# Causal attention scores: two float32r products over 128 rows in place of one native float32 product over 64

## The chip, the cores and the metric

The kernel runs on one core of a Trainium2 chip. The metric is device time in microseconds (us) for one execution, the median of three. In the rows, PE is TensorE (PEld its weight loads), DVE VectorE, ACT ScalarE, POOL GpSimd and SP SyncE, which issues the weight transfers.

## The reference, cut to what matters

Two layers on 256 tokens of 1024 features. Each layer is a half-step SwiGLU FFN, a mixer and another half-step FFN. All of it is float32. The mixer runs two attentions on the same normalised input: NSA (8 query heads, 2 key groups, with a compressed, a selected and a window branch under per-head gates) and MoBA (8 heads with keys of their own).

```python
x = x + 0.5 * _swiglu(_rms(x, ffn1_norm[l]), ...)
h = _rms(x, mix_norm[l])
(q_a, g_a, kc, vc, ks_, vs_, kw, vw, q_b, k_b, v_b, gate_a, gate_b) = _split_cols(h @ w_in[l])
y_a = _nsa(...) @ w_branch_nsa[l]
y_b = _moba(q_b, k_b, v_b) @ w_branch_moba[l]
x = x + (jax.nn.sigmoid(gate_a) * y_a + jax.nn.sigmoid(gate_b) * y_b) @ w_out[l]
x = x + 0.5 * _swiglu(_rms(x, ffn2_norm[l]), ...)
# in _nsa; selected and window branch alike, and MoBA per head:
s = jnp.einsum('grqd,gqnkd->grqnk', qc, kg) * scale
p = _masked_softmax(s, mask, (-2, -1))
return jnp.einsum('grqnk,gqnkd->grqd', p.astype(vg.dtype), vg)
```

At 256 tokens the selected blocks, the window and MoBA's one block hold every token up to the query's own. So three attentions are plain causal ones over 64-wide heads, and NSA's selected and window branch share their queries and differ in keys and values (the two key sets).

## The kernel before, in words

**Weights.** They come in pieces of [128, 2048] float32 on SP's queue, three raw buffers deep. ACT casts each half piece to float32r (`split_hi`, L218), DVE subtracts to get the remainder (`split_lo`, L225). A float32r operand holds the high part of a float32; its remainder is a second operand. Every large product is three float32r products (`mm3`, L133): high by high, high by low, low by high.

**Order.** The program is written out in the order of emission; no scheduler moves it. `tick` (L140) runs after every `mm3`: it emits deferred work (`defer`), a weight split every third tick, and every third tick one step of the attention (`side_step`), a generator that waits for flags. So PE sees nine weight products, then one step of the attention, then nine products. Each engine works its queue in order.

**The attention of one layer.** `cb_rope` rotates queries and keys on DVE right after their projection (L464 to L473). `pairs_T` (L513) transposes them on PE, two heads to a transpose of 128 columns, four transposes to a PSUM bank, and ACT copies the bank to SBUF as float32. `attend` (L680) makes jobs: token tile 0 has 4 heads to a score bank (128 keys each), tile 1 has 2 heads (256 keys). A job has three stages, and `attend_all` (L637) puts into one step the scores of job i, the transposes of the probabilities of job i-1 and the value products of job i-2:

- s1: native float32 score products over the 64 rows of a head (L695), mask (L698), maximum (L700), and on ACT an exponential for each head (L703), which gives P;
- s2: transposes of P (L711), which ACT copies (L713);
- s3: products with the values (L720); after the last head the gate weights (L538 to L542) and the scaling on DVE.

NSA has 16 heads per tile (8 for either key set): 4 score banks for tile 0 and 8 for tile 1. MoBA has 2 and 4. `compressed` (L646) is a job of its own behind each NSA tile: scores over 15 compressed keys (L652), a softmax written out on DVE (L655 to L662) with one exponential on ACT, `cpt` (a transpose) and `co` (its value product). The projections that run meanwhile are the output gates and MoBA's q, k and v.

**Buffers.** Tiles of 8 KB per partition come from a ring of 14 (`s4`, L92). PSUM has two banks for each of four uses: long sums a0 and a1, transposes `tr`, scores `sc`.

Of the kernel before, what the change touches and what calls it, by code (L numbers as in the profile page):

```python
# [39 lines left out]


def constants():
    """Position tables and masks: they depend on shapes alone."""
# [19 lines left out]
    # sums the halves' rows (half, g, c) of the compressed hidden layer, for keys and for values  # L63
# [17 lines left out]
def hybrid_kernel(ctx: ExitStack, tc: tile.TileContext, T, out):  # L81
# [9 lines left out]

    def s4(name, shape, dt=F32):  # L92
        return p4.tile(shape, dt, name=name, tag="s4", bufs=14)
# [21 lines left out]
    def flush():  # L115
        while later and later[0][0] <= clock[0]:
# [12 lines left out]
    def side_until(flag):  # L129
        while flag not in flags:  # L130
            assert side_step(), flag

    def mm3(ps, x, w, start, stop):  # L133
        """One [128, 128] block of float32 activations times [128, N] of weights, in exact halves."""
# [71 lines left out]
    # the splits' order: halves of a piece, finer for the first piece  # L206
# [33 lines left out]
    def get(*keys):  # L240
        """The halves of the named pieces, the first of which is the oldest still in use."""
# [39 lines left out]
    kbd = const.tile([128, G, 2, 16], F32, name="kbd")  # L281
    nc.gpsimd.memset(kbd, 0.0)
# [10 lines left out]
    class Norm:  # L293
# [7 lines left out]
        def squares(self, t, c, n, i):  # L301
            """The i-th share of the sum of squares, from n features"""
# [3 lines left out]
        def trans(self, t, h, wait=1):  # L306
            """The transpose's halves of the tokens t, features h, scaled by the gains"""
# [13 lines left out]
        def root(self, t, n):  # L321
            """r = rsqrt(mean(x^2) + eps): a power, and a step of Newton's"""
# [20 lines left out]
    def transposes(pair, src):  # L343
        """[128 tokens, n * 128] -> its transpose's halves, [128, n, 128] each"""
# [22 lines left out]
    def finish(nrm, g, y, t, h, ps):  # L367
        """x += ps / 2, and the output's share"""
# [19 lines left out]
    def ffn(l, n, nrm):  # L388
        actT = []
# [4 lines left out]
        for f in range(F // 512):  # L394
            hl = [s4("aT" + nm, [128, 4, S], F32R) for nm in "hl"]
            actT += [[y[:, k] for y in hl] for k in range(4)]
# [17 lines left out]
        # the last 256: gates and ups side by side  # L414
        aT = s4("aT", [128, 2, 2, S], F32R)
        hl = [aT[:, j] for j in range(2)]
# [33 lines left out]
        for t in range(NT):  # L450
            for h in range(2):
# [4 lines left out]
                else:  # L456
                    residual(nxt, t, h, ps[t][h], 4 + t)
        return nxt

    def rope(dst, ps, r, t, n, tab, dup):  # L460
        """dst [128, n, (dup,) 64] = rope(r * ps [128, n, 64]) at token tile t."""
# [7 lines left out]
        if dup:  # L469
            nc.vector.tensor_add(dst, t1[:, :, None, :].to_broadcast([128, n, 2, HD]),  # L470
                                 t2[:, :, None, :].to_broadcast([128, n, 2, HD]))
        else:
            nc.vector.tensor_add(dst, t1, t2)  # L473

    def mixer(l, nrm):
        # small weights of the compressed branch, a row (half, dim) per partition
# [29 lines left out]
        qa = s4("qa", [128, NT, NH, HD])  # L506
        # compressed blocks: the dims (half, d) by position, then (keys or values, high or low, g, c)
# [384 lines left out]
```

## Time and profile before

| | |
|---|---|
| median of three runs | 1198.42 us (1197.92 to 1198.84) |
| span of the profiled execution | 1195.6 us |
| PE busy | 1180.3 us, 99% of the span |
| DVE, ACT, POOL busy | 713.7 (60%), 577.9 (48%), 32.2 us (3%) |
| granted TensorE clock, mean | 0.998 of full speed |
| transfers | 203.5 MB, 170 GB/s on average |

The span is what the profiler saw from the first to the last instruction, 2.8 us less than the median of the runs. Busy time of PE includes fill and drain of each product, which overlap with the next; the distance between two starts tells what a product costs in a stream.

### The profile page before, as it was taken

How to read it: one execution, taken by the hardware profiler on the slowest of the kernel's cores; microseconds unless marked ns; L12 is line 12 of the kernel's file. 1: busy time of each engine (PE TensorE's matmuls, PEld its weight loads, DVE VectorE, ACT ScalarE, POOL GpSimd, SP SyncE). 2: the span in 40 equal slices, each digit the busy share in tenths (PEclk: the TensorE clock that was granted, in tenths of full speed). 3: DMA queues.
4: the chain of work that ended last, by engine and by line, in shares of the span. 5: the costliest groups of instructions: out<-in, count | busy, mean ns of one | idle time of the engine just before them, and what ended most of it. 6: DMA issues, size and time to landing. Idle time of an engine off the chain costs nothing.

```text
span 1195.6 us, 14342 instructions
## 1 busy us (share of the span) xinstructions
PE 1180.3 (99%) x5685; PEld 974.3 (81%) x5685; DVE 713.7 (60%) x976; ACT 577.9 (48%) x911; POOL 32.2 (3%) x41
## 2 busy tenths in 40 slices
PE   7999999999999999999999999999999999999997
PEld 5888888987878888888888888888878788888885
DVE  6655546877647674555475455487765576655553
ACT  6544444465456364444355444346545555444332
POOL 1000000001100000000000000000001000000000
PEclk9999999999999999999999999999999999999999
DMA  7756463763243466555546555537424254755540
GB/s 262 249 172 209 142 243 89 202 212 106 89 158 108 156 225 192 192 169 202 197 148 205 188 194 185 188 116 211 160 91 131 97 177 136 251 176 179 187 180 35
DMA packets 103282, 203.52 MB, mean 170 GB/s; under 512 B 4496, under 2 KB 25184, under 8 KB 103216
## 3 DMA queue, kind: packets, MB, share of 16 engines
q1 hardware_dynamic: 102592, 201.77, 51.5%
q8 instruction: 44, 0.72, 0.3%
q10 hardware_dynamic: 384, 0.55, 0.1%
q0 software_dynamic: 240, 0.30, 0.1%
q14 instruction: 22, 0.18, 0.0%
HBM read 201.55 MB, written 1.05 MB: 169 GB/s over the span
## 4 chain that ended last, share of the span: by engine, by line
PE 98%; DMA 1%; issue 0%; DVE 0%; ACT 0%; SPq 0%; POOLq 0%; POOL 0%
PE pr L135 9%; PE pr L137 8%; PE pr L136 8%; PE dn L137 7%; PE dn L135 7%; PE dn L136 7%; PE u L135 6%; PE u L136 6%; PE u L137 6%; PE g L136 6%; PE g L135 6%; PE g L137 6%; PE s L695 3%; PE o L720 3%; PE pT L349 2%; PE pt L711 2%
## 5 line engine op out<-in xcount | busy, mean ns | idle before, releaser
L225 DVE TENSOR_TENSOR lo<-raw,hi 128x1024 fp32r<-128x1024 f32 (+3 forms) x386 | 454.9, 1204 | 190.8 <-ACT hi L218 190.5
L218 ACT CAST hi<-raw 128x1024 fp32r<-128x1024 f32 (+3 forms) x386 | 386.5, 1038 | 227.2 <-PE dn L137 92.8
L135 PE MATMUL g<-hi,hT 128*128 128x512 f32 x320 | 129.3, 404 | 1.1 <-ACT hi L218 1.1
L135 PE MATMUL pr<-hi,hT 128*128 128x512 f32 (+2 forms) x320 | 129.7, 405 | 0.0
L136 PE MATMUL g<-lo,hT 128*128 128x512 f32 x320 | 125.5, 392 | 0.3 <-DVE lo L225 0.3
L135 PE MATMUL dn<-hi,aTh 128*128 128x512 f32 x320 | 125.8, 393 | 0.0
L137 PE MATMUL g<-hi,hT 128*128 128x512 f32 x320 | 125.5, 392 | 0.0
L137 PE MATMUL dn<-hi,aTl 128*128 128x512 f32 x320 | 124.7, 390 | 0.0
L135 PE MATMUL u<-hi,hT 128*128 128x512 f32 x320 | 124.6, 389 | 0.0
L136 PE MATMUL u<-lo,hT 128*128 128x512 f32 x320 | 124.5, 389 | 0.0
L136 PE MATMUL dn<-lo,aTh 128*128 128x512 f32 x320 | 124.5, 389 | 0.0
L137 PE MATMUL u<-hi,hT 128*128 128x512 f32 x320 | 124.5, 389 | 0.0
L137 PE MATMUL pr<-hi,hT 128*128 128x512 f32 (+2 forms) x320 | 122.6, 383 | 0.0
L136 PE MATMUL pr<-lo,hT 128*128 128x512 f32 (+2 forms) x320 | 121.8, 381 | 0.0
L703 ACT ACTIVATE P<-s,m 128x128 f32<-128x128 f32 (+1 forms) x96 | 39.4, 419 | 73.1 <-DVE m L700 53.0
L351 DVE TENSOR_TENSOR aTl<-pT,aTh 128x512 fp32r<-128x512 f32 x40 | 27.7, 692 | 76.2 <-ACT aTh L350 76.2
L136 PEld LDWEIGHTS g<-lo,hT 128*128 128x128 f32 x320 | 60.6, 189 | 12.8 <-DVE lo L225 1.3
L135 PEld LDWEIGHTS g<-hi,hT 128*128 128x128 f32 x320 | 60.5, 189 | 12.7 <-ACT hi L218 1.5
L137 PEld LDWEIGHTS g<-hi,hT 128*128 128x128 f32 x320 | 60.4, 189 | 12.8
L137 PEld LDWEIGHTS dn<-hi,aTl 128*128 128x128 f32 x320 | 60.1, 188 | 12.6
L135 PEld LDWEIGHTS u<-hi,hT 128*128 128x128 f32 x320 | 60.1, 188 | 12.5
L137 PEld LDWEIGHTS u<-hi,hT 128*128 128x128 f32 x320 | 60.1, 188 | 12.5
(193 smaller groups left out, 1585.4 us busy)
## 6 DMA issues: line engine op xcount, KB each, us to landing
raw<-in_ffn_wd SPq DMA_DIRECT2D x44, 1024.0 KB, 5.0
raw<-in_ffn_wu SPq DMA_DIRECT2D x40, 1024.0 KB, 5.1
raw<-in_ffn_wg SPq DMA_DIRECT2D x38, 1024.0 KB, 5.1
raw<-in_w_in SPq DMA_DIRECT2D x32, 1024.0 KB, 5.0
raw<-in_w_out SPq DMA_DIRECT2D x8, 1024.0 KB, 5.2
raw<-in_ffn_wg SPq DMA_DIRECT2D x12, 512.0 KB, 4.0
raw<-in_ffn_wu SPq DMA_DIRECT2D x8, 512.0 KB, 5.0
raw<-in_w_branch_nsa SPq DMA_DIRECT2D x4, 1024.0 KB, 5.1
```

Source lines behind the costliest of these rows:

```text
L135: nc.tensor.matmul(ps, x[0], w[0], start=start, stop=False)
L136: nc.tensor.matmul(ps, x[0], w[1], start=False, stop=False)
L137: nc.tensor.matmul(ps, x[1], w[0], start=False, stop=stop)
L218: nc.scalar.copy(done[i][0][:, a], raws[i][:, a])
L225: nc.vector.tensor_sub(lo[:, a], raws[i][:, a], hi[:, a].bitcast(F32))
L349: nc.tensor.transpose(p[:, k], src[:, 128 * k:128 * k + 128], ident)
L351: defer(1, lambda: nc.vector.tensor_sub(lo, p, hi.bitcast(F32)))
L695: nc.tensor.matmul(sp[:, i], qT[r, h // 2, 128 * t:128 * t + 128], kT(h)[r, 0:128 * nk], start=True, stop=True)
L703: nc.scalar.activation(P[:, i].rearrange("p a b -> p (a b)"), sp[:, i], AF.Exp, bias=m[:, i:i + 1], accum_out=O["su"][:, h:h + 1])
L711: nc.tensor.transpose(pt[:, i * nk + c], st["P"][:, i, c], ident)
L720: nc.tensor.matmul(O["o"][:, h], st["pT"][:, i * nk + c], v(h, c), start=c == 0, stop=c == nk - 1)
```

## The change

The scores are computed from float32r halves. A query's high part lies on 64 rows and its remainder on the other 64; the keys' high parts lie twice, on both halves, and so do the keys' remainders. Two products over 128 rows, one with each, then add up in PSUM (`start=u == 0`). For NSA one product serves both key sets at once, so its bank holds items (head, key set) and its columns are doubled: 512 for tile 1, 256 for tile 0. MoBA has 256 and 128.

For this the rotation of the queries ends in a split (add on DVE, cast on ACT, remainder on DVE), `queries_T` transposes one head at a time, `keys_T` writes high part and remainder, and two key banks go into one step. MoBA's keys are written twice by the rotation. The gates of both key sets are applied at once to a group's four heads. Compressed scores become eight float32r products with the high part and remainder of the keys side by side, summed on DVE. `s4` gets 15 named slots that are given back by hand, a flag is raised two ticks after its projection, and `kbd` is no longer zeroed on POOL.

```diff
+    slots, held = list(range(15)), {}
-        return p4.tile(shape, dt, name=name, tag="s4", bufs=14)
+        i = slots.pop(0)
+        a = p4.tile(shape, dt, name=name, tag=f"s4_{i}", bufs=1)
+        held[id(a)] = i, a
+        return a
+    def drop(*tiles):
+        slots.extend(held.pop(id(a))[0] for a in tiles)
...
@@ rope
+        if split:
+            nc.vector.tensor_add(t1, t1, t2)
+            nc.scalar.copy(dst[:, :, 0], t1)
+            defer(1, lambda: nc.vector.tensor_sub(dst[:, :, 1], t1, dst[:, :, 0].bitcast(F32)))
...
@@ mixer
-            flags.add((l, flag))
+            defer(2, lambda: flags.add((l, flag)))
-        def pairs_T(src, n, d, need=None):
-            for a in range(0, n, 2):
-                p = bank("tr", "pQ", [128, 2, S])
+        def queries_T(src, d):
+            for t in range(NT):
+                d.append(s4("qT", [128, NH, 128], F32R))
+                for a in range(0, NH, 4):
+                    p = bank("tr", "pQ", [128, 4, 128])
+                    for i in range(4):
+                        nc.tensor.transpose(p[:, i], src[t][:, a + i].rearrange("p u d -> p (u d)").bitcast(F32), ident)
+                    nc.scalar.copy(d[t][:, a:a + 4], p)
+                drop(src[t])
+                yield None
+        def keys_T(src, pairs, hi, lo):
+            for a in range(pairs):
+                p = bank("tr", "pK2", [128, 2, S])
...
+                h = hi(a)
+                nc.scalar.copy(h, p)
+                defer(1, lambda a=a, h=h, p=p: nc.vector.tensor_sub(lo(a), p, h.bitcast(F32)))
+                if a % 2:
+                    yield None
...
@@ compressed, s1
-                for a in range(4):
-                    nc.tensor.matmul(sp[:, 2 * a:2 * a + 2, :], qT[:, a, 128 * t:128 * t + 128], kbd[:, a // 2],
-                                     start=True, stop=True)
+                for h in range(NH):
+                    nc.tensor.matmul(sp[:, h], qT[t][:, h], kbd[:, h // 4], start=True, stop=True)
-                nc.vector.tensor_add(s, sp, K["cneg"][:, t, None, :].to_broadcast([128, NH, 16]))
+                nc.vector.tensor_add(s, sp[:, :, 0], K["cneg"][:, t, None, :].to_broadcast([128, NH, 16]))
+                nc.vector.tensor_add(s, s, sp[:, :, 1])
...
@@ attend, s1
-                    for i, h in enumerate(heads):
-                        r = slice(64 * (h % 2), 64 * (h % 2) + 64)
-                        nc.tensor.matmul(sp[:, i], qT[r, h // 2, 128 * t:128 * t + 128], kT(h)[r, 0:128 * nk],
-                                         start=True, stop=True)
+                    for i in range(0, per, nj):
+                        h = some[i][0]
+                        for u in range(2):
+                            nc.tensor.matmul(sp[:, i:i + nj], qT[t][:, h], kT(h, u, 128 * nk), start=u == 0, stop=u == 1)
...
@@ attention
-            yield from pairs_T(ksd.rearrange("p t j g u d -> p t (j g) (u d)"), 4, ksT)
+            yield from keys_T(lambda t, i: ksd[:, t, i % 2, i // 2], G, lambda g: ks[0][:, g], lambda g: ks[1][:, g])
...
-            yield from pairs_T(qa.rearrange("p t (a u) d -> p t a (u d)", u=2), 4, qaT)
+            yield from queries_T(qa, qaT)
...
+                        a = scaled("aS", o, weights_of(su, gate[:, t, hs, 1:3])).rearrange("p (h j) d -> p h j d", j=2)
+                        nc.gpsimd.tensor_add(A[:, t, hs], a[:, :, 0], a[:, :, 1])
...
-            yield from pairs_T(qb[0].rearrange("p t (a u) d -> p t a (u d)", u=2), 4, qbT)
-            yield from pairs_T(kb[0].rearrange("p t (a u) d -> p t a (u d)", u=2), 4, kbT)
+            yield from queries_T(qb, qbT)
+            yield from keys_T(lambda t, i: kb[t][:, i], NH // 2, lambda a: half(0, a), lambda a: half(1, a))
```

How the queues stand after it. DVE, around the compressed softmax of NSA tile 0 in the first layer, before (`rt` and `qb` are the rotation of MoBA's first query tile, `cs` the compressed scores, `lo` a weight remainder, the last row the mask of the first bank of tile 1):

```order
L473 TENSOR_TENSOR qb<-rt_2190,rt_2192 128x512
L225 TENSOR_TENSOR lo<-raw,hi 128x1024
L655 TENSOR_TENSOR cs_2213<-cs,c_cneg 128x128
L657 TENSOR_REDUCE cm<-cs_2213 128x8
L658 TENSOR_TENSOR cs_2213<-cs_2213,cm 128x128
L660 TENSOR_TENSOR cs_2213<-cs_2213,c_cok 128x128
L662 TENSOR_REDUCE csu<-cs_2213 128x8
L539 TENSOR_SCALAR cf<-csu 128x8
L540 RECIPROCAL cf<-cf 128x8
L542 TENSOR_TENSOR cf<-cf,gate 128x8
L225 TENSOR_TENSOR lo<-raw,hi 128x1024
L698 TENSOR_TENSOR s<-s,c_causal 128x2x128
```

And after the change:

```order
L695 TENSOR_TENSOR cs_2222<-cs_2222,cm 128x128
L697 TENSOR_TENSOR cs_2222<-cs_2222,c_cok 128x128
L699 TENSOR_REDUCE csu<-cs_2222 128x8
L571 TENSOR_SCALAR cf<-csu 128x8
L572 RECIPROCAL cf<-cf 128x8
L578 TENSOR_TENSOR cf<-cf,gate 128x8
L477 SCALAR_TENSOR_TENSOR rt_2248<-pr,r,ropeq 128x512
L481 SCALAR_TENSOR_TENSOR rt_2250<-pr,r,ropeq 128x8x32 x2
L483 TENSOR_TENSOR rt_2248<-rt_2248,rt_2250 128x512
L485 TENSOR_TENSOR qb<-rt_2248,qb 128x8x64
L236 TENSOR_TENSOR lo<-raw,hi 128x1024
L735 TENSOR_TENSOR s<-s,c_causal 128x2x128
```

The rotation (`rt`, `qb`) stood ahead of the compressed softmax and stands behind it now, between it and the mask of the next bank, and its last row needs ACT's cast.

ACT at the same place, before (`P` is a bank's exponentials, `pT` the copy of its transposes, `cpT` that of the compressed ones, `hi` a weight cast):

```order
L218 CAST hi<-raw 128x1024
L659 ACTIVATE cs_2213<-cs_2213 128x128
L713 COPY pT<-pt 128x512
L703 ACTIVATE P,su<-s,m 128x256 x2
L669 COPY cpT<-cpt 128x128
L218 CAST hi<-raw 128x1024
L703 ACTIVATE P,su<-s,m 128x256 x2
```

And after:

```order
L229 CAST hi<-raw 128x1024
L696 ACTIVATE cs_2222<-cs_2222 128x128
L750 COPY pT<-pt 128x512
L484 CAST qb<-rt_2248 128x8x64
L229 CAST hi<-raw 128x1024
L740 ACTIVATE P,su<-s,m 128x256 x2
L706 COPY cpT<-cpt 128x128
L740 ACTIVATE P,su<-s,m 128x256 x2
L750 COPY pT<-pt 128x512
```

The casts of the two query tiles (`qb`) are new; the weight cast and the exponentials of the next banks of tile 1 stand behind them.

## Rows read from the trace of the kernel before

**Rows 1.** The page: part 1 (busy us, share, instructions), part 4 (share of the chain).
```profile
PE 1180.3 (99%) x5685; PEld 974.3 (81%) x5685; DVE 713.7 (60%) x976; ACT 577.9 (48%) x911; POOL 32.2 (3%) x41
...
PE 98%; DMA 1%; issue 0%; DVE 0%; ACT 0%; SPq 0%; POOLq 0%; POOL 0%
```

**Rows 2.** PE's timeline in the attention: start us, us, engine line op out<-in xcount.
```profile
261.29 0.40 PE L137 MATMUL pr<-hi,hT 128*128 128x512 f32 x1
...
262.71 0.65 PE L711 MATMUL pt<-c_ident,P 128*128 128x128 f32 x4
...
274.58 0.97 PE L652 MATMUL cs<-kbd,qaT 128*128 128x32 f32 x8
275.39 0.64 PE L711 MATMUL pt<-c_ident,P 128*128 128x128 f32 x4
...
278.60 0.39 PE L137 MATMUL pr<-hi,hT 128*128 128x512 f32 x1
278.92 1.13 PE L695 MATMUL s<-ksT,qaT 64*128 64x256 f32 x4
279.98 0.33 PE L667 MATMUL cpt<-c_ident,cs 128*128 128x128 f32 x1
...
284.28 0.66 PE L711 MATMUL pt<-c_ident,P 128*128 128x128 f32 x4
...
293.49 0.66 PE L711 MATMUL pt<-c_ident,P 128*128 128x128 f32 x4
```

**Rows 3.** The same timeline of PE around the hidden layer of the compressed branch.
```profile
241.54 0.40 PE L137 MATMUL pr<-hi,hT 128*128 128x512 f32 x1
241.77 0.28 PE L630 MATMUL hh<-hi,X 128*128 128x256 f32 x1
241.89 0.27 PE L630 MATMUL hh<-lo,X 128*128 128x256 f32 x1
...
246.02 0.60 PE L519 MATMUL pQ<-c_ident,qa 128*128 128x128 f32 x4
246.37 0.48 PE L135 MATMUL pr<-hi,hT 128*128 128x512 f32 x1
246.69 0.39 PE L136 MATMUL pr<-lo,hT 128*128 128x512 f32 x1
```

**Rows 4.** The timeline of DVE around the compressed softmax of NSA tile 0.
```profile
273.88 0.74 DVE L464 SCALAR_TENSOR_TENSOR rt<-pr,r,ropeq 128x512 f32<-128x512 f32 x1
...
276.05 1.22 DVE L225 TENSOR_TENSOR lo<-raw,hi 128x1024 fp32r<-128x1024 f32 x1
277.18 0.28 DVE L655 TENSOR_TENSOR cs<-cs,c_cneg 128x128 f32<-128x128 f32 x1
...
279.66 1.22 DVE L225 TENSOR_TENSOR lo<-raw,hi 128x1024 fp32r<-128x1024 f32 x1
280.80 0.43 DVE L698 TENSOR_TENSOR s<-s,c_causal 128x256 f32<-128x256 f32 x1
281.26 0.69 DVE L700 TENSOR_REDUCE m<-s 128x2 f32<-128x512 f32 x1
281.86 0.16 DVE L539 TENSOR_SCALAR cf<-su 128x8 f32<-128x8 f32 x1
...
282.57 0.69 DVE L533 TENSOR_TENSOR aS<-o,cf 128x512 f32<-128x512 f32 x1
```

**Rows 5.** The timeline of ACT: two of the exponentials.
```profile
262.25 0.21 ACT L703 ACTIVATION_READ_ACCUMULATOR P<-s,m 128x1 f32 x1
...
282.06 0.47 ACT L703 ACTIVATE P<-s,m 128x256 f32<-128x256 f32 x1 [3.13 <-DVE cf L539]
```

**Rows 6.** Groups by line, DVE and ACT: form xcount | busy us, mean ns | idle before.
```profile
L351 DVE TENSOR_TENSOR sl<-pT,sh 128x512 fp32r<-128x512 f32 x8 | 5.5, 690 | 8.2 <-ACT sh L350 8.2
...
L350 ACT CAST sh<-pT 128x512 fp32r<-128x512 f32 x8 | 4.7, 588 | 17.9 <-PE pT L349 17.9
```

**Rows 7.** Stretch: us, PE, PEld, DVE, ACT, POOL busy (x), clock, DMA share, GB/s.
```profile
258.00:320.00 62.00, 62.00 (x352) 49.16 (x350) 43.19 (x81) 32.71 (x94) 3.39 (x2) 1.00 0.27 86
```

More of the change, by code (lines that the diff above doesn't have):

```diff
@@ L113, in defer, with flush @@
         later.sort(key=lambda e: e[0])
-    def flush():
-        while later and later[0][0] <= clock[0]:
+    def flush(ahead=0):
+        while later and later[0][0] <= clock[0] + ahead:
             later.pop(0)[1]()
@@ L457, in ffn, with rope @@
                     residual(nxt, t, h, ps[t][h], 4 + t)
+        drop(*tiles)
         return nxt
-    def rope(dst, ps, r, t, n, tab, dup):
+    def rope(dst, ps, r, t, n, tab, split):
         C = tab[:, t, None, 0:HD].to_broadcast([128, n, HD])
@@ L505, in mixer @@
         vv = p2.tile([128, NT, 2, G * HD], F32, name="vv", tag="vv", bufs=1)
-        qa = s4("qa", [128, NT, NH, HD])
+        qa = [s4("qa", [128, NH, 2, HD], F32R) for _ in range(NT)]
         X2 = [s4("X2", [128, 8, 2, 2, G, 16], F32R) for _ in range(2)]
@@ L541, in weights_of @@
             if gt is not None:
-                nc.vector.tensor_mul(c, c, gt)
+                if len(gt.shape) == 3:
+                    c2 = c.rearrange("p (h j) -> p h j", j=2)
+                    nc.vector.tensor_mul(c2, c2, gt)
+                else:
+                    nc.vector.tensor_mul(c, c, gt)
             return c
@@ L616, in compress_more @@
             nc.tensor.transpose(kp.rearrange("p g c -> p (g c)"), kc2.rearrange("p u d -> p (u d)"), ident[:64, :64])
-            for u in range(2):
-                r = slice(64 * u, 64 * u + 64)
-                nc.scalar.copy(kbd[r, :, u, :], kp[r, :, 0:16])
+            nc.scalar.copy(kbd[:, :, 0], kp[:, :, 0:16])
+            nc.vector.tensor_sub(kbd[:, :, 1], kp[:, :, 0:16], kbd[:, :, 0].bitcast(F32))
         HH = sm.tile([128, 2, CMP_HIDDEN], F32, name="HH", bufs=1)
@@ L634, in hidden @@
             nc.scalar.copy(HH, ps)
+            drop(*X2)
             flags.add((l, "HH"))
@@ L676, in compressed, with attend, s1 @@
             return s1, s2_, s3
-        HEADS = [0, 2, 4, 6, 1, 3, 5, 7]
-        def attend(t, qT, kT, v, finish):
+        def attend(t, heads, nj, qT, kT, v, finish):
             nk = t + 1
             per = 4 // nk
+            items = [(h, j) for h in heads for j in range(nj)]
             O = {}
-            for h0 in range(0, NH, per):
-                heads = HEADS[h0:h0 + per]
+            for i0 in range(0, len(items), per):
+                some = items[i0:i0 + per]
                 st = {}
-                def s1(h0=h0, heads=heads, st=st):
-                    if h0 == 0:
+                def s1(i0=i0, some=some, st=st):
+                    if i0 == 0:
                         O["su"] = sm.tile([128, NH], F32, name="su")
                     sp = bank("sc", "s", [128, per, 128 * nk])
-                    for i, h in enumerate(heads):
-                        r = slice(64 * (h % 2), 64 * (h % 2) + 64)
-                        nc.tensor.matmul(sp[:, i], qT[r, h // 2, 128 * t:128 * t + 128], kT(h)[r, 0:128 * nk],
-                                         start=True, stop=True)
+                    for i in range(0, per, nj):
+                        h = some[i][0]
+                        for u in range(2):
+                            nc.tensor.matmul(sp[:, i:i + nj], qT[t][:, h], kT(h, u, 128 * nk), start=u == 0, stop=u == 1)
                     own = sp[:, :, 128 * t:128 * t + 128]
@@ L701, in s1 @@
                     P = s2("P", [128, per, nk, 128])
-                    for i, h in enumerate(heads):
+                    for i in range(per):
                         nc.scalar.activation(P[:, i].rearrange("p a b -> p (a b)"), sp[:, i], AF.Exp,
-                                             bias=m[:, i:i + 1], accum_out=O["su"][:, h:h + 1])
+                                             bias=m[:, i:i + 1], accum_out=O["su"][:, i0 + i:i0 + i + 1])
                     st["P"] = P
@@ L713, in s2_, with s3 @@
                     nc.scalar.copy(st["pT"], pt)
-                def s3(h0=h0, heads=heads, st=st):
-                    if h0 == 0:
+                def s3(i0=i0, some=some, st=st):
+                    if i0 == 0:
                         O["o"] = bank("a1", "o", [128, NH, HD])
-                    for i, h in enumerate(heads):
+                    for i, (h, j) in enumerate(some):
                         for c in range(nk):
-                            nc.tensor.matmul(O["o"][:, h], st["pT"][:, i * nk + c], v(h, c),
+                            nc.tensor.matmul(O["o"][:, i0 + i], st["pT"][:, i * nk + c], v(h, c, j),
                                              start=c == 0, stop=c == nk - 1)
-                    if h0 + per == NH:
+                    if i0 + per == len(items):
                         finish(O["o"], O["su"])
@@ L812, in mixer @@
             elif c0 == C_Q:
-                project_in(c0, cb_rope(qa, ropeq), "Q")
+                project_in(c0, cb_rope(lambda t: qa[t], ropeq, True), "Q")
             elif c0 == C_QB:
-                project_in(c0, cb_rope(qb[0], ropeq))
+                qb.extend(s4("qb", [128, NH, 2, HD], F32R) for _ in range(NT))
+                project_in(c0, cb_rope(lambda t: qb[t], ropeq, True))
             elif c0 == C_KB:
-                kb.append(s4("kb", [128, NT, NH, HD]))
-                project_in(c0, cb_rope(kb[0], K["rope"]), "KB")
+                kb.extend(s4("kb", [128, NH, 2, HD]) for _ in range(NT))
+                project_in(c0, cb_rope(lambda t: kb[t], K["rope"], False), "KB")
             else:
```

65 lines of the change are left out of this document (36 added, 29 removed).

## The prediction

> **What bounds the kernel now.** I read the page first: TensorE (PE) is busy for 99% of the span, and the chain of work that ended last is PE for 98% [rows 1]. So a microsecond taken from PE is a microsecond of the run, as long as nothing else becomes late, and the reader should keep two lists: what each PE instruction costs in its place, and how early the results arrive that PE will ask for. For the first I read the timeline of PE around a side step of the attention [rows 2], and around the hidden layer [rows 3], where float32r products of 256 columns run. A record's duration contains its fill and drain and overlaps the next one, so I price by the distance from one start to the next. For the second I read the timelines of VectorE (DVE) and ScalarE (ACT) in the same stretch [rows 4, 5], and the stretch's totals: DVE is busy 43 of 62 us, ACT 33, and the granted clock is 1.00, that is 2.4 GHz [rows 7].
>
> The profiled execution has a span of 1195.6 us; the median of the three runs is 1198.42 us, 2.8 us more. I subtract what follows from the median.
>
> **Part 1: the score products (gain).** A native float32 product over 64 rows leaves two records (x4 for the two heads at 278.92 [rows 2]). A bank of token tile 1 (two heads, 256 keys): from the last ordinary product at 278.60 to what follows the scores at 279.98 are 1.38 us, of which 0.23 us is the ordinary product itself [rows 2, 3]; the scores cost 1.15 us, a gap of 0.09 us ahead of them included. Ahead of the float32r products of 256 columns there is no such gap (241.54 to 241.77 is 0.23 us), and each costs 0.12 us [rows 3]. A bank of tile 0 (four heads, 128 keys): 261.29 to 262.71 less 0.23 is 1.19 us [rows 2]. After the change, per layer:
> - NSA, tile 1: 8 banks, two products of 512 columns each, 2 x 0.23 = 0.46 us. Saved 8 x 0.69 = 5.5 us.
> - NSA, tile 0: 4 banks, four products of 256 columns, 0.48 us. Saved 4 x 0.71 = 2.8 us.
> - MoBA, tile 1: 4 banks, four products of 256 columns. Saved 4 x 0.67 = 2.7 us.
> - MoBA, tile 0: 2 banks, eight products of only 128 columns. The trace has no float32r product this narrow. Low end: half of a 256-column one, 0.06 us. High end: a native one, 1.19 us less the gap for four, 0.27 us each. I take 0.11 us, the distance of the 128-column transposes (0.35 us for four, and what they delay behind them [rows 3]), since these too load new stationary data every time. 8 x 0.11 = 0.88 us; saved 2 x 0.31 = 0.6 us. The ends give +1.4 and -2.0 us.
> - Compressed scores: eight records before (0.81 us, 274.58 to 275.39 [rows 2]), eight products after; taken as 0, within 0.3 us.
>
> Sum 11.6 us per layer, 23.2 us for both.
>
> A place where a page differs: the transposes of 128 columns stand 0.11 us apart [rows 3]. The Trainium skill (TensorE: Matmul & The Clock Gate, section Back-to-back issue gap) gives about 81 ns for each of a stream of 128-column products and about 131 ns at 512 columns; by it the four MoBA banks of tile 0 would save another 0.9 us. The trace's 512-column products stand 0.23 us apart, not 0.13, so I stay with the rows.
>
> **Part 2: more transposes (loss).** Queries: 16 transposes where there were 8, for NSA and for MoBA; MoBA keys 16 for 8; NSA keys unchanged. That is 24 more per layer, 6 groups of four. A group at 246.02 delays the second ordinary product after it to 246.69; 0.67 less 0.23 is 0.44 us [rows 3]. 6 x 0.44 = 2.6 us per layer, 5.3 us in all. They are matched by copies out of PSUM at 0.59 us each on ACT and subtractions at 0.69 us on DVE [rows 6]: per layer ACT gets 10 more (four query halves, four query banks, two key banks), DVE four query remainders and six key remainders, two wider additions for the MoBA keys, and an addition per compressed tile. DVE has 19 us to spare in the 62 us [rows 7], so throughput is hidden; where they stand in the queue is not (part 3). Where two banks are transposed in one step, the next pair waits for both copies: 0.87 us of transposes and nine products (2.1 us) cover 1.2 us of copies, one weight split and the remainders. I cost these bank waits at nothing; without that cover it would be about 0.3 us at five places a layer.
>
> **Part 3: what is late next (loss).** PE now reaches the transposes of the probabilities P 0.7 us sooner at each step, while the softmax behind them isn't shorter.
> - First bank of NSA tile 0. Its last P ends at 262.46 (262.25 plus 0.21), the last of the four transposes starts 0.33 us after 262.71 [rows 2, 5]: 0.58 us to spare. The way there loses the 0.71 us of the next bank's scores and the 0.1 us gap behind its own. Wait: 0.3 us. In MoBA tile 0 the scores shrink by 0.3 us alone: none.
> - First bank of NSA tile 1. Here the order shows the trap. The NSA keys take one step fewer, so the attention runs a step ahead of the projections. The MoBA query rotation, which DVE did ahead of the compressed softmax, now lands between it and the scores of this bank, and it ends in a round trip: DVE adds, ACT casts, DVE subtracts. DVE, counted from the start of the compressed scores: 1.0 us until they can be read; the compressed softmax 2.5 us (277.18 to 279.66) plus 0.3 for the new addition; rotation 2.2 (273.88 to 276.05); cast and remainder 0.59 + 0.69 and two handovers, 1.4; weight remainder 1.1; mask 0.5; maximum to first P 0.8 [rows 4, 5, 6]; P itself 0.5. Sum 10.3 us. PE: 274.58 to 278.92 less the gap of 0.09, then 278.92 to 284.28 less 2 x 0.69 [rows 2]: 8.2 us. Wait: 2.1 us, and 0.2 more for the second P. Before, that P was done at 282.53 (282.06 plus 0.47), 1.75 us early.
> - Two steps on, the second query tile does it again. From that first P on, DVE owes gate weights 0.7, a scaling 0.6, weight remainder 1.1, mask and maximum 1.1, the compressed scaling 0.6, rotation 2.2, round trip 1.4, mask to first P 1.8: 9.5 us, less the 0.5 between maximum and transpose, 9.0. PE: 284.28 to 293.49 is 9.2, less 2 x 0.69, plus 0.2: 8.0 us. Wait: 1.0 us.
>
> Queued behind the cast on ACT are a weight cast and the P of the next bank; behind the remainder on DVE a weight remainder and the next mask. PE waits for both chains.
>
> Sum 3.6 us per layer, 7.2 us in all. Its lower end is nothing, if the handovers and the weight remainders fall better; its upper end 4.5 us per layer, with the bank waits.
>
> **Sum.** 23.2 - 5.3 - 7.2 = 10.7 us: 1198.4 - 10.7 = **1187.7 us**.
>
> **The rivals.**
> - A: no new waits. For it: DVE and ACT are busy 70% and 53% of the stretch [rows 7], and later banks leave time. Against it: the queue order above. 1198.4 - 17.9 = 1180.5 us.
> - B: float32r products of 128 columns run at the native pace of 0.27 us. For it: no row shows one. Against it: at 256 columns a float32r product costs 0.12 us [rows 3]. It takes 2.6 us per layer from part 1, and gives 1187.7 + 5.2 = 1192.9 us.
> - C, slower: the round trip DVE, ACT, DVE sets the pace of the attention instead of PE, so that PE waits at every bank of NSA tile 1. It decides from 8.95 us of waits per layer, 1.1 us at each of eight banks. At 1.5 us per bank it gives 1180.5 + 24 = 1204.5 us. For it: two of the banks wait 1 to 2 us already. Against it: the round trip is met only where a query rotation falls, twice in the stretch, and DVE idles 30% of it [rows 7].
> - D: the change doesn't do what it says, and a float32r product over 128 rows with these operands costs as much as a native one. Then each bank doubles, and 1.15 us are added at some 16 banks per layer: 1198.4 + 5.3 + 37 = 1241 us. The hidden layer's rows [rows 3] speak against it.
>
> **How the numbers follow.** Forecast with its waits (1184 to 1191) 0.61; A 0.17; B 0.14; C 0.06; D 0.02. The range holds the forecast, A and B, with their unknowns: 1180 to 1194 us. A measurement of this kernel can tell about 0.2%, 2.4 us: faster means under 1196.0, slower above 1200.8. The forecast, A and B with no more than 0.01 lost are faster: 0.91. C and D, less a little of C that ends level, are slower: 0.06. The same: 0.03.
>
> **What would show it.** In the profile after: score records half as many per product, 0.23 us apart at 512 columns and 0.12 at 256; at 128 columns 0.11 (B: 0.27). 24 more transposes per layer. Idle time of PE ahead of the P transposes, put down to ACT P, of some 7 us in total, the longest about 2 us at the first bank of NSA tile 1 in each layer; A if there is none, C if it stands at all eight banks. The page should still have PE at 98 to 99% and the FFNs unchanged. I am wrong if the span shrinks by under 4 us or over 19, or if the waits stand elsewhere, such as at PSUM banks of the transposes.

## The result, and the profile after

The changed kernel takes 1189.27 us (median of four runs, 1187.61 to 1191.56) where the kernel before takes 1198.32 beside it: a ratio of 0.9928, 95% interval 0.9916 to 0.9941. A second set of five runs gave 1189.18 us (1187.39 to 1189.95). The prediction was 1187.7, with a range of 1180 to 1194.

The profiled execution took 1187.61 us, with a span of 1185.5 us where before's was 1195.6. The page of after, parts 1 and 4, which answer to [rows 1]:

```profile
PE 1165.1 (98%) x5669; PEld 973.2 (82%) x5669; DVE 730.1 (62%) x1002; ACT 587.6 (50%) x929; POOL 37.4 (3%) x44
...
PE 95%; DVE 2%; ACT 1%; DMA 1%; issue 1%; SPq 0%; POOLq 0%; POOL 0%; ACTq 0%; DVEq 0%
```

PE is busy for 15.2 us less while the span shrank by 10.1, and the chain now runs through DVE and ACT for some 3%. So PE waits where it did not before. PE's timeline after, in the same stretch of layer 0 as [rows 2] (start, us, group; in brackets the idle time ahead of it and its releaser):

```profile
271.53 0.96 PE L689 MATMUL cs<-kbd,qT 128*128 128x32 f32 x8
272.34 0.66 PE L748 MATMUL pt<-c_ident,P 128*128 128x128 f32 x4
...
275.81 0.62 PE L733 MATMUL s<-ksT,qT 128*128 128x512 f32 x2
276.27 0.27 PE L704 MATMUL cpt<-c_ident,cs 128*128 128x128 f32 x1
...
279.35 0.62 PE L733 MATMUL s<-ksT,qT 128*128 128x512 f32 x2
281.88 0.90 PE L748 MATMUL pt<-c_ident,P 128*128 128x128 f32 x4 [1.91 <-ACT P L740]
282.62 1.02 PE L710 MATMUL co<-vbd,cpT 128*128 128x512 f32 x2
...
289.43 0.61 PE L733 MATMUL s<-ksT,qT 128*128 128x512 f32 x2
290.63 0.89 PE L748 MATMUL pt<-c_ident,P 128*128 128x128 f32 x4 [0.59 <-ACT P L740]
```

A bank's scores cost 0.46 us (275.81 to 276.27). At 279.35 and 289.43 the same two products are followed by 2.53 and 1.20 us: waits of 2.07 and 0.74 us for the first P. The transposes of P behind the first (`pt`) stretch to 0.74 us (281.88 to 282.62) from 0.43 elsewhere, since the bank's second P is 0.3 us later still.

The table of PE's waits in the whole run (us, times, longest), of PE and of its weight loads:

```profile
PE pt L748 <- ACT P L740: 4.4, 3, 1.9
```
```profile
PEld pt L748 <- ACT P L740: 8.0, 12, 2.3
PEld o L757 <- ACT pT L750: 1.7, 6, 0.3
```

No bank of the transposes of queries and keys (pQ, pK) stands in it. The stretch of [rows 7] after (us, then busy us of PE, PEld, DVE, ACT and POOL; granted clock, DMA share, GB/s) has 2.7 us less of PE and 5.1 more of DVE, at the same clock:

```profile
258.00:320.00 62.00, 59.31 (x337) 48.86 (x336) 48.27 (x92) 34.75 (x96) 7.80 (x5) 1.00 0.30 100
```

DVE in the same place, to be read against [rows 4]:

```profile
275.33 0.74 DVE L477 SCALAR_TENSOR_TENSOR rt<-pr,r,ropeq 128x512 f32<-128x512 f32 x1
275.99 0.87 DVE L481 SCALAR_TENSOR_TENSOR rt<-pr,r,ropeq 128x256 f32<-128x256 f32 x2
276.90 0.69 DVE L483 TENSOR_TENSOR rt<-rt,rt 128x512 f32<-128x512 f32 x1
278.27 0.69 DVE L485 TENSOR_TENSOR qb<-rt,qb 128x512 fp32r<-128x512 f32 x1 [0.69 <-ACT qb L484]
278.88 1.22 DVE L236 TENSOR_TENSOR lo<-raw,hi 128x1024 fp32r<-128x1024 f32 x1
280.02 0.43 DVE L735 TENSOR_TENSOR s<-s,c_causal 128x256 f32<-128x256 f32 x1
```

The bank scored at 275.81 was written at 276.4, but its mask starts at 280.02, and its P is what PE waits for until 281.88. Rotation, 0.69 us of idling for ACT's cast, the remainder and a weight remainder stand ahead of it. The same idling of 0.69 us comes back at the second query tile (288.16).

### The profile page after: what moved, and what is told of

Read it like the earlier page. It is cut to its first block, busy times and chain, and to the rows that moved or that the text cites. A ratio compares the mean times of both kernels' runs of the same rounds, so it can differ in the third digit from the quotient of the medians.

```text
span 1185.5 us, 14381 instructions
## 1 busy us (share of the span) xinstructions
PE 1165.1 (98%) x5669; PEld 973.2 (82%) x5669; DVE 730.1 (62%) x1002; ACT 587.6 (50%) x929; POOL 37.4 (3%) x44
## 4 chain that ended last, share of the span: by engine, by line
PE 95%; DVE 2%; ACT 1%; DMA 1%; issue 1%; SPq 0%; POOLq 0%; POOL 0%; ACTq 0%; DVEq 0%
PE pr L146 8%; PE pr L148 8%; PE pr L147 8%; PE dn L146 7%; PE dn L147 7%; PE dn L148 7%; PE u L146 6%; PE u L147 6%; PE u L148 6%; PE g L147 6%; PE g L148 6%; PE g L146 6%; PE o L757 2%; PE pT L359 2%; PE s L733 1%; PE pt L748 1%
## 5 line engine op out<-in xcount | busy, mean ns | idle before, releaser
L148 PEld LDWEIGHTS u<-hi,hT 128*128 128x128 f32 x320 | 60.1, 188 | 12.5
L146 PEld LDWEIGHTS u<-hi,hT 128*128 128x128 f32 x320 | 60.1, 188 | 12.5
L147 PEld LDWEIGHTS u<-lo,hT 128*128 128x128 f32 x320 | 60.1, 188 | 12.4
```

The source lines that it names most:

```text
L146: nc.tensor.matmul(ps, x[0], w[0], start=start, stop=False)
L147: nc.tensor.matmul(ps, x[0], w[1], start=False, stop=False)
L148: nc.tensor.matmul(ps, x[1], w[0], start=False, stop=stop)
```

## Experiments

The first theory, Q: the waits come from what DVE has queued between the compressed scores and the mask of the next bank, and an edit that takes x us out of that queue takes x us off the wait. Rival S: the shorter scores alone make PE wait. Rival R: the round trip DVE, ACT, DVE is the whole price. And, for the runs' spread, a clock theory: a long wait lets the granted clock fall in some executions.

**The keys in two steps.** The attention falls back one step against the projections, as it stood before the change:

```diff
-                if a % 2:
+                if a % 2 or pairs == 2:
                     yield None
```

> The NSA keys yield after each bank again, so the attention falls back to where it stood against the projections before the change; the scores, the transposes and the round trip of the queries' split stay. Theory Q (queue): the waits of TensorE at the first banks of NSA tile 1 (2.36 and 1.25 us in layer 0) come from what DVE has queued between the compressed scores and the mask, and any edit that takes x us out of that queue takes x us off the wait. Here the MoBA query rotation starts about 1.7 us sooner against the compressed scores, so the first wait falls from 2.4 to about 0.6 us, some 4 us in both layers: 1189.3 - 4 = 1185 us (1183 to 1187). Rival S (scores): TensorE waits because its scores are shorter, wherever the rotation stands: the waits stay within 0.5 us, 1188.5 to 1190. Rival R (round trip): the cast on ACT and the handovers are what is late; the rotation's place matters little and the wait goes along with it: 1188 to 1190. Clock: if the spread of the changed kernel (1187.6 to 1191.6, mean granted clock 0.998 to 0.996) comes from waits of over 2 us, the runs of this kernel agree within 1.5 us at 0.998.

Measured: 1190.8 us median (1188.2 to 1191.62), no gain, where theory Q as I had put it gave 1183 to 1187. PE's timeline of this kernel shows why:

```profile
277.90 0.61 PE L733 MATMUL s<-ksT,qT 128*128 128x512 f32 x2
279.82 0.30 PE L704 MATMUL cpt<-c_ident,cs 128*128 128x128 f32 x1 [1.31 <-DVE cs L697]
...
282.96 0.62 PE L733 MATMUL s<-ksT,qT 128*128 128x512 f32 x2
283.55 0.90 PE L748 MATMUL pt<-c_ident,P 128*128 128x128 f32 x4
...
287.21 0.61 PE L733 MATMUL s<-ksT,qT 128*128 128x512 f32 x2
289.45 0.89 PE L748 MATMUL pt<-c_ident,P 128*128 128x128 f32 x4 [1.62 <-ACT P L740]
```

The wait of 2.07 us for the first P is down to 0.13 (282.96 to 283.55 is 0.59, less 0.46). But the rotation now stands ahead of the compressed softmax, and `cpt` waits for that instead: 277.90 to 279.82 is 1.92, less 0.46, 1.46 us. The second rotation falls between two masks and costs 1.78 us (289.45 less 287.21 less 0.46) where it cost 0.74. So the place of the rotation against the projections decides where the waits stand; here it did not lessen their sum, since at both new places PE wanted a result from behind it in DVE's queue.

**The remainder on GpSimd.**

```diff
-            defer(1, lambda: nc.vector.tensor_sub(dst[:, :, 1], t1, dst[:, :, 0].bitcast(F32)))
+            defer(1, lambda: nc.gpsimd.tensor_sub(dst[:, :, 1], t1, dst[:, :, 0].bitcast(F32)))
```

> The remainder of the rotated queries (sum less cast) is formed on GpSimd, not on DVE; DVE keeps the addition, ACT the cast. Theory Q (queue): DVE loses the 0.69 us for which it stands idle for the cast and the 0.6 us of the subtraction, 1.3 us at each query rotation. The waits fall from 2.36 to 1.05 us and from 1.25 to nothing, the later 0.68 us to 0.2 to 0.6: some 2.6 us per layer, 1189.3 - 5.2 = 1184 us (1182.5 to 1186). Rival S (the shorter scores alone): nothing moves, 1188.5 to 1190. Rival R (the round trip is the whole price): both waits vanish, 3.6 us per layer, 1182 us. GpSimd's subtraction is not waited for, since the transposes of these queries come several steps later. Clock: no stretch under 1.00 and runs within 1.5 us of each other, if no wait of 2 us is left.

Measured: 1184.48 us (1183.5 to 1185.21), 0.9884 of before (0.987 to 0.9897), as theory Q had it. The wait at the first bank of NSA tile 1:

```profile
280.54 0.62 PE L733 MATMUL s<-ksT,qT 128*128 128x512 f32 x2
281.69 0.89 PE L748 MATMUL pt<-c_ident,P 128*128 128x128 f32 x4 [0.54 <-ACT P L740]
```

It is 0.69 us (1.15 less 0.46), 1.4 us less; the wait of 0.74 at the second query tile is gone. Rival S falls. Of the 4.8 us between the medians some is clock: against the changed kernel's executions at a mean clock of 0.998 (1187.4 to 1187.6) the gain is 2.2 to 4.1 us. The edit also moves the NSA queries' remainder, and projection products (`pr`) of this kernel cost 309.5 us in all, against 308.6 of the changed kernel, which speaks for a price of GpSimd there.

**No round trip at all.** The remainders of the MoBA queries are left out, so ACT's cast goes as well:

```diff
+        if bare:
+            nc.vector.tensor_add(dst[:, :, 0], t1, t2)
+            nc.gpsimd.memset(dst[:, :, 1].bitcast(F32), 0.0)
```

> The MoBA queries are written as a high part alone: DVE's addition writes it rounded, GpSimd zeroes the other half, and neither cast nor subtraction is made; the remainders of the MoBA queries are left out of the computation. Theory Q (queue): as with the remainder on GpSimd, 1.3 us less of DVE's queue at each rotation, and ACT is also free of a cast of 0.6 us: 1183 to 1185 us, within 1.5 us of the kernel with the remainder on GpSimd. Rival R (the round trip is the whole price): both waits vanish, 1182 us or less. Rival S (the shorter scores alone): 1188.5 to 1190. A difference between this kernel and the one with the remainder on GpSimd is the price of ACT's cast.

Measured: 1183.34 us (1182.46 to 1183.7). The first wait is the same as with the remainder on GpSimd (0.70 us), so rival R, by which it would vanish, falls. What the 1.1 us between the two medians pay for is not shown: this kernel also has the NSA queries' remainder back on DVE, and in the profiled executions 0.9 us of the difference stand at projection products (309.5 to 308.6 us).

**Both edits.** The keys in two steps, and the remainder on GpSimd.

> Both edits at once: the NSA keys yield after each bank, and the remainders of the rotated queries are formed on GpSimd. Theory Q (queue): 1.7 + 1.3 us is more than the 2.36 us of the first wait, and the 1.3 us cover the second, so waits of at most 0.5 us per layer are left: 1181 to 1183 us, the sum without waits being 1180.5. If the order and the round trip were two names for one thing, this gives no more than the better of the two alone (1184). Rival S: 1188.5 to 1190. Clock: all runs within 1.5 us, mean granted clock 0.998.

Measured: 1185.97 us (1185.18 to 1186.04), 1.5 us more than the remainder on GpSimd alone; the 1181 to 1183 us of theory Q missed: the two edits do not add up. That the attention runs a step ahead is a small gain, not the trap that I took it for.

**The changed kernel again**, on the chip of the next two experiments.

> The changed kernel itself once more, beside the others on one chip. Clock theory: its runs stray between 1187.6 and 1191.6 us because a wait of over 2 us in the attention lets the granted clock fall for a while in some executions; so the runs here stray by 3 us or more again, the longer ones at a lower mean granted clock (0.996 against 0.998), each 0.001 of mean clock being worth about 1.2 us of the span or more. Rival: the spread was chance, and five runs agree within 1.5 us at one clock.

Measured: 1187.39 and 1187.42 us at a mean granted clock of 0.998, 1189.18, 1189.29 and 1189.95 at 0.997. With the first set (1187.61 at 0.998; 1189.24 and 1189.3 at 0.997; 1191.56 at 0.996) all nine runs line up by their clock, some 2 us for each 0.001. The five runs stray by 2.6 us, a little less than the 3 us expected. The order by clock does not hold for every kernel: with the remainder on GpSimd the two runs at 0.998 took 1183.5 and 1183.9 us, the two at 0.999 took 1185.1 and 1185.2. So up to 1.7 us of spread have other causes, which were not followed.

**DVE time put back.** The remainder on GpSimd as above, and behind each query cast two additions that nobody reads:

```diff
+            if True:
+                for _ in range(2):
+                    nc.vector.tensor_add(idle, x[:, 0, 0:512], x[:, 0, 0:512])
```

> The remainders on GpSimd as in the kernel that reached 1184.5 us, and in their place on DVE two idle additions of 128x512 (nothing reads them) behind each query tile's cast, 1.4 us, about what the idle time for the cast and the subtraction had taken. Theory Q (queue): only the time in DVE's queue counts, not the round trip: the waits come back as they were (2.4 and 1.2 us in layer 0), 1188 to 1191 us, and the spread of over 3 us with them. Rival R (the round trip itself, its casts and handovers, is what costs): 1184 to 1186.

Measured: 1195.16 us (1193.89 to 1196.15), well above what theory Q gave. DVE, PE and GpSimd of this kernel at the first MoBA query tile:

```profile
279.41 1.41 DVE L489 TENSOR_TENSOR idle<-x 128x512 f32<-128x512 f32 x2
280.73 2.32 DVE L236 TENSOR_TENSOR lo<-raw,hi 128x1024 fp32r<-128x1024 f32 x1
```
```profile
284.83 0.89 PE L752 MATMUL pt<-c_ident,P 128*128 128x128 f32 x4 [2.96 <-ACT P L744]
```
```profile
280.22 1.74 POOL L486 TENSOR_TENSOR qb<-rt,qb 128x512 fp32r<-128x512 f32 x1 [5.53 <-ACT qb L485]
```

From start to start the additions cost 1.32 us (279.41 to 280.73), and the weight remainder 2.25 (to the mask at 282.98) where it costs 1.14 in the changed kernel (278.88 to 280.02), while GpSimd's subtraction runs beside it until 281.96. Together 2.4 us more; the wait at that bank went from 0.69 to 3.12 us (scores at 281.25, `pt` at 284.83, less 0.46), 2.4 us. So time in DVE's queue alone, with no round trip in it, brings the wait back one for one. The rest of the 10.7 us over the kernel with the remainder on GpSimd lies at the other rotations and in the clock (below): the second MoBA query tile waits 0.70 us again in layer 0, and behind the NSA query rotation a projection product waits 1.24 us (222.15) for the next rotation on DVE, in a part of the layer that theory Q had not looked at.

**Longer still.** Three such additions at the first query tiles of the changed kernel.

> Three idle additions of 128x512 on DVE (nothing reads their result) stand behind the cast of each first query tile, 3 x 0.69 us = 2.1 us more in DVE's queue per layer where the wait of 2.36 us is. Theory Q (queue): that wait grows by what the 0.69 us of idle time there does not swallow, 1.4 to 2.1 us per layer. With the clock unmoved that is 1187.6 + 2.8 to 4.2 = 1190.4 to 1191.8. Clock theory: waits of 4 us let the granted clock fall in every execution, as it did behind the second wait of the kernel with two key steps (0.71 for some 9 us, about 3.5 us lost): 1194 to 1199 us, a mean granted clock of 0.995 or less and a stretch at about 0.7 in the windows behind the wait. Rival: the additions are hidden and nothing moves, 1187.6 to 1191.6.

Measured: 1196.23 us (1195.76 to 1197.5), every run at a mean clock of 0.994 or 0.995. The two stretches at and behind the wait in layer 0 (columns as above), and PE's timeline there:

```profile
282.00:288.00 6.00, 3.13 (x8) 1.84 (x9) 5.67 (x11) 1.39 (x6) 1.64 (x1) 0.67 0.05 7
288.00:294.00 6.00, 6.00 (x28) 5.00 (x27) 3.41 (x7) 2.67 (x7) 1.28 (x1) 0.76 0.47 168
```
```profile
284.87 1.14 PE L752 MATMUL pt<-c_ident,P 128*128 128x128 f32 x4 [3.20 <-ACT P L744]
...
288.79 0.63 PE L146 MATMUL pr<-hi,hT 128*128 128x512 f32 x1
289.22 0.63 PE L147 MATMUL pr<-lo,hT 128*128 128x512 f32 x1
```

Behind the wait the products of 512 columns stand 0.43 us apart (288.79 to 289.22) in place of 0.23: PE runs at the lower of its two levels, 1.2 GHz, until 290.8, and then at 2.4 again. The wait itself grew by 1.29 us (idle time 3.20 against 1.91), just under the 1.4 to 2.1 that theory Q gave. By their mean clocks all eleven runs lost time as the clock theory has it; but in the trace the same idle time of 3.20 us in layer 1 (872.80) left the clock at 1.00.

**The subtraction alone moved.** The MoBA queries' remainder (`later_by` is 4 for them, 1 for NSA's) stays on DVE, three ticks later and so behind the next mask:

```diff
-            defer(1, lambda: nc.vector.tensor_sub(dst[:, :, 1], t1, dst[:, :, 0].bitcast(F32)))
+            defer(later_by, lambda: nc.vector.tensor_sub(dst[:, :, 1], t1, dst[:, :, 0].bitcast(F32)))
```

> Only the subtraction of the MoBA queries' remainder is emitted three ticks later, so that it stands behind the next bank's mask and maximum in DVE's queue, and ACT's cast has long been done by then. DVE's work is the same; nothing goes to GpSimd. Theory Q in its present form (what counts is the time that DVE's queue holds between the compressed scores and the mask of the next bank, idle time in it included): 0.69 us of idling and 0.6 us of subtracting leave that place, as they did with the subtraction on GpSimd, and the 0.6 us come back one bank later, where there is room. The first wait falls from 2.1 us to about 0.75, the second from 0.7 to 0.2 to 0.4: 1184 to 1186 us. Rival W (the amount of DVE's work counts, wherever it stands): 1187.5 to 1189.5, as the changed kernel.

Measured: 1185.86 us (1185.59 to 1186.58). DVE's work is unchanged, and the median is 3.3 us below that of the changed kernel's second set; against that set's executions at a mean clock of 0.998 (1187.4) the gain is 0.8 to 1.8 us. The first wait is 0.70 us, as with GpSimd; at the bank behind it a wait of 0.54 us is new, somewhat more than the 0.2 to 0.4 expected. Rival W, by which only the amount of DVE's work counts, falls by the first wait above all.

**The mask first.** The whole rotation of the MoBA queries is emitted four ticks later, and so behind the mask:

```diff
-                project_in(c0, cb_rope(lambda t: qb[t], ropeq, True))
+                late = cb_rope(lambda t: qb[t], ropeq, True)
+                project_in(c0, lambda t, ps: defer(4, lambda: late(t, ps)))
```

> The whole rotation of the MoBA queries is emitted four ticks later, so that the mask and maximum of the first bank of NSA tile 1 stand ahead of it on DVE; cast and remainder stay behind it. Theory Q: the first wait (2.1 us) vanishes, but mask, gate weights, scaling, rotation, round trip, weight remainder and the next mask now all fall between the first and the second bank: by the rows that P would be 1.8 us late. One wait of 1.8 us in place of 2.1 and 0.7: a gain of about 1.2 us per layer, 1185 to 1187.5 us, with the wait at the bank one step later. Rival: moving the rotation behind the mask takes the wait away altogether, 1182 to 1184. Rival W (DVE's work): no change, 1187.5 to 1189.5.

Measured: 1188.2 us (1187.63 to 1188.79). PE's timeline:

```profile
279.26 0.63 PE L733 MATMUL s<-ksT,qT 128*128 128x512 f32 x2
279.72 0.60 PE L748 MATMUL pt<-c_ident,P 128*128 128x128 f32 x4
...
283.11 0.62 PE L733 MATMUL s<-ksT,qT 128*128 128x512 f32 x2
285.31 0.89 PE L748 MATMUL pt<-c_ident,P 128*128 128x128 f32 x4 [1.58 <-ACT P L740]
```

The first bank waits for nothing, the second for 1.74 us (2.20 less 0.46), where 1.8 had been worked out. The time is 0.7 us above the range that I had given, and inside rival W's 1187.5 to 1189.5; the timeline and not the time speaks for Q here. All five runs had a mean clock of 0.997: behind the same wait in layer 1 the granted clock was 0.69 and 0.75 for two stretches of 3 us, by which 1.7 us were lost (3 x 0.31 + 3 x 0.25).

```profile
867.00:870.00 3.00, 2.96 (x14) 2.44 (x15) 0.43 (x1) 2.80 (x7) 0.78 (x1) 0.69 0.71 270
870.00:873.00 3.00, 3.00 (x14) 2.44 (x13) 0.20 (x1) 0.00 (x0) 0.00 (x0) 0.75 0.00 0
```

**The mask first, and the remainder on GpSimd.**

> Both: the MoBA query rotation four ticks later, behind the mask of the first bank of NSA tile 1, and its remainder on GpSimd. Theory Q: the wait of 1.8 us that the later rotation alone leaves at the second bank loses the round trip's 1.3 us, some 0.6 us stay there, 0.3 at the key rotation: 1182.5 to 1184 us, the least of all kernels that compute the whole reference. Rival P (GpSimd's subtraction holds DVE's weight remainder up, as where it took 2.32 us in place of 1.22 beside it): 1184.5 to 1186.

Measured: 1183.98 us (1183.2 to 1184.32), 0.9881 of before (0.9866 to 0.9897), the least of all that compute the whole reference, though its lead of 0.5 us on GpSimd's subtraction alone is within both intervals. The second bank's wait is down to 0.36 us (283.74 to 284.56 less 0.46); below it the table of the waits of PE's weight loads:

```profile
283.74 0.62 PE L733 MATMUL s<-ksT,qT 128*128 128x512 f32 x2
284.56 0.90 PE L748 MATMUL pt<-c_ident,P 128*128 128x128 f32 x4 [0.20 <-ACT P L740]
```
```profile
PEld pt L748 <- ACT P L740: 3.3, 10, 0.6
```

**High part by DVE, the rest on GpSimd.**

```diff
+            nc.vector.tensor_add(dst[:, :, 0], t1, t2)
+            nc.gpsimd.tensor_add(t1, t1, t2)
+            nc.gpsimd.tensor_sub(dst[:, :, 1], t1, dst[:, :, 0].bitcast(F32))
```

> DVE's addition writes the rotated queries' high part at once; GpSimd forms the sum again and subtracts, so neither DVE nor ACT has any part in the remainder and nothing is left out. Theory Q (queue): as the kernel without remainders, 1183.3 us (1182.3 to 1184.3), about 1 us under the one with GpSimd's subtraction behind ACT's cast. Rival P: GpSimd's two operations, some 3.2 us per tile by the 1.6 us that its subtraction took, hold the buffers of the rotation and DVE waits for them: 1184.5 to 1187.

Measured: 1186.6 us (1186.26 to 1187.57), 2 us worse than one operation on GpSimd, as rival P had it, though by another way than the rotation's buffers. DVE and GpSimd of this kernel:

```profile
282.05 1.07 DVE L576 TENSOR_TENSOR cf<-cf,gate 128x8 f32<-128x8 f32 x1
```
```profile
281.82 1.27 POOL L485 TENSOR_TENSOR qb<-rt,qb 128x512 fp32r<-128x512 f32 x1
```

A gate product of 128x8 elements, 0.17 us in the changed kernel (281.52), takes 1.07 us beside GpSimd's subtraction, and ends with it at 283.1. The next bank's P is late by it: PE waits 0.35 us there, where with one operation on GpSimd it waited for nothing.

## Why the prediction was right, point by point

I added up all distances from one PE start to the next, by operation, in the profiled executions of before and after. Scores: 38.3 to 23.6 us; projection products: 312.6 to 308.6, of which 3.2 are the gap of 0.09 us ahead of 34 banks of the old scores; transposes of queries and keys: 7.1 to 12.5; transposes of P (`pt`): 17.2 to 19.2; value products (`o`): 29.2 to 29.9. Together these are -14.7 - 4.0 + 5.4 + 2.0 + 0.7 = -10.6 us.

- **Part 1, 23.2 us predicted.** The prices held. In after, two products of 512 columns take 0.46 us, four of 256 columns 0.47 or 0.48, and the eight of 128 columns 0.84 us, 0.105 each, where I had taken 0.11 from the transposes; the rows are below. Without waits the scores come to 16 x 0.46 + 16 x 0.47 + 4 x 0.84 = 18.2 us, so 38.3 - 18.2 + 3.2 (the gaps) = 23.3 us were won. The compressed scores cost 0.81 us (271.53 to 272.34), as before. Rival B, native pace at 128 columns, and rival D are out.
- **Part 2, 5.3 us predicted.** 64 pQ and 64 pK stand in after where 80 stood before, 24 more per layer; 12.5 - 7.1 = 5.4 us. The bank waits that I took as nothing do not show in the table of waits.
- **Part 3, 7.2 us predicted.** The scores' 23.6 us are 5.4 over their 18.2; `pt` and `o` grew by 2.0 and 0.7: 8.1 us in all, within the upper end of 9.0. Layer 0 (distances less 0.46, 0.43 or 0.81): first bank of NSA tile 0 0.40, where 0.3 was put down (its own terms, 0.71 + 0.1 - 0.58, give 0.23); first bank of NSA tile 1 2.07 + 0.31, against 2.1 + 0.2; second query tile 0.74 + 0.51, against 1.0. I had not counted the MoBA key rotation (0.68, behind the scores at 302.40) and MoBA's first bank of tile 1 (0.32, at 348.98). In layer 1 the second query tile waits for nothing, which I had not looked for. DVE's timeline shows why: there the second rotation (870.08, the rows are below) stands behind the mask of the bank (869.00), in layer 0 ahead of it (285.23 against 288.77). So it is partly luck that the sum came near: two waits that were not counted stand against one in layer 1 that was counted and is not there.
- **The reason that I gave for part 3** was half right. At the first bank of NSA tile 1 the chain of DVE work held to a tenth of a microsecond (271.53 to 281.88 is 10.35, against 10.3); at the second query tile it held to a quarter in layer 0 (281.88 to 290.63 is 8.75, against 9.0) and failed in layer 1. That the attention runs a step ahead decides where the waits stand, not their size: set back by a step, they stand elsewhere and sum to no less.
- **Rival C** is out by size: the round trip sets the pace at two banks, not at eight. **Rival A** would need DVE's queue emptied; the best version found still waits 3.3 us for P, by the table of PE's weight loads.

The sum gives 23.3 + 0.8 (the rest of the projection products, which the prediction did not have) - 5.4 - 8.1 = 10.6 us, against 10.7 forecast; the span shrank by 10.1, and most of the half microsecond between is at the FFN's gate products (225.7 to 226.4 us), which was not followed. The executions at a mean clock of 0.998 took 1187.4 to 1187.6 us, on the forecast of 1187.7. The median is 1.6 us above it, and six of the nine runs have a lower mean clock, a term that the prediction did not have; that they lose it behind a wait is inferred (see the last section).

The rows of PE's timeline after for two banks of part 3, and for the 128 columns of part 1 (a bank of MoBA's tile 0):

```profile
260.80 1.08 PE L748 MATMUL pt<-c_ident,P 128*128 128x128 f32 x4
261.63 0.48 PE L146 MATMUL pr<-hi,hT 128*128 128x512 f32 x1
...
302.40 0.62 PE L733 MATMUL s<-ksT,qT 128*128 128x512 f32 x2
303.04 0.90 PE L748 MATMUL pt<-c_ident,P 128*128 128x128 f32 x4
303.97 1.10 PE L757 MATMUL o<-vv,pT 128*128 128x64 f32 x8
...
345.13 1.01 PE L733 MATMUL s<-kbT,qT 128*128 128x128 f32 x8
345.97 0.62 PE L748 MATMUL pt<-c_ident,P 128*128 128x128 f32 x4
```

260.80 to 261.63 is 0.83 us for four transposes that take 0.43 elsewhere; 302.40 to 303.04 is 0.18 more than the two products, and 303.04 to 303.97 0.50 more than the transposes. 345.13 to 345.97 is 0.84 us for eight products.

And DVE's in layer 1, where the mask of the third bank of NSA tile 1 comes ahead of the second rotation:

```profile
869.00 0.43 DVE L735 TENSOR_TENSOR s<-s,c_causal 128x256 f32<-128x256 f32 x1 [0.96 <-PE s L733]
870.08 0.74 DVE L477 SCALAR_TENSOR_TENSOR rt<-pr,r,ropeq 128x512 f32<-128x512 f32 x1
```

## What to carry to other kernels

Where one engine is busy for 99% of the span, price a faster product by the distance from start to start, and then follow the queue of the engine that must answer it: here some 23 us won on PE became 10, since 5 went into new transposes and 8 into waits. Within an in-order queue count everything that stands between the arrival of the scores and the instruction that reads them, idle time for another engine's part in it included. Moving the whole rotation to another place of the same dense stretch mostly moved the wait; what helped was to take a part of it off the engine, or to put it where nobody waits behind it, as the subtraction moved behind the mask and layer 1's second rotation show. A wait on TensorE can cost more than its length, since the clock may fall behind it.

## What the runs showed of the hardware

**The clock behind a wait.** The kernel with two key steps, in the profiled run, behind its wait of 1.78 us at 289.45:

```profile
288.00:294.00 6.00, 4.49 (x17) 3.63 (x18) 4.68 (x7) 4.75 (x12) 2.12 (x1) 0.71 0.05 9
294.00:300.00 6.00, 6.00 (x27) 4.95 (x26) 1.78 (x3) 1.85 (x7) 0.00 (x0) 0.72 0.49 169
```

That run took 1191.62 us; the fastest of the same kernel, at a mean clock of 0.998, took 1188.2. The 3.4 us between them are what 12 us at 0.715 lose (12 x 0.285 = 3.4). Yet in both profiled runs of the changed kernel a wait of 2.07 us left the granted clock at 1.00, and with DVE time put back a wait of 3.1 us in layer 0 did too, while in layer 1 of that run the clock was 0.72 from 870 to 876. The length of the wait alone does not decide, and what does, these runs do not show. Nor is it the same in every run of a kernel: the nine runs of the changed kernel have mean clocks from 0.996 to 0.998. That its slower runs lost their time behind these waits is inferred from their mean clocks and from the other kernels' traces: neither of its profiled runs shows a drop. The Trainium skill (TensorE: Matmul & The Clock Gate, section Part 1: The HAM clock gate) says of the clock's rise at a kernel's start that the same kernel measures a different number of matmuls at the lower clock from run to run; no run here shows that count.

**DVE and GpSimd hold each other up.** A weight remainder took 2.32 us beside GpSimd's subtraction and 1.22 alone, a gate product 1.07 and 0.17. The other way round, GpSimd's addition in the kernel with two operations there took 2.12 us beside a weight remainder that had started first (279.63 behind 279.38), and 1.30 at the second query tile. The Trainium skill (SBUF — State Buffer, section SBUF: two separate sides) has the two engines share a pair of ports, which whoever starts first keeps for the whole instruction, against a VectorE operation with two SBUF inputs too. By that the remainder would end about one duration after GpSimd's end at 281.96; it ended at 283.05, 1.09 later. The trace agrees.
